# Weight sums moved from GpSimd to VectorE, and a pair's raw weights fetched in the middle of the pair before it

## The chip, the cores and the metric

One core of a Trainium2 chip runs the whole kernel in one launch. The metric is the device time of one execution in microseconds (us). Three runs of the kernel before took 2743.4, 2746.61 and 2750.3 us; the median is 2746.61.

The engines are TensorE (PE), VectorE (DVE), ScalarE (ACT), GpSimd (POOL) and SyncE (SP), which here issues the transfers (DMA). Each runs its own instructions in order and waits for the others by semaphores.

## The reference

One layer of a diffusion backbone over 1024 tokens of width 1024, all in fp32: a half SwiGLU feed-forward, then a token mixing of two branches (a bidirectional matrix LSTM with 4 heads, and a chunked spatial gating) that share one combined input projection, then a second half SwiGLU feed-forward and a final norm.

```
def project(h, shift, scale, g, w_in, sizes):
    hn = modulate(rmsnorm(h, g), shift, scale)
    return split_cols(hn @ w_in[:, :sum(sizes)], sizes)
...
p_lat = project(h, mods[3], mods[4], g_mix[layer], w_in[layer], PROJ_SIZES)
```

`mods` are nine vectors of shifts, scales and gates, made from the conditioning vector by one large product with `w_ada`. The change lies in the combined projection: q, k, v, the gate columns, o, u, vs and two merge gates ga and gb, each 1024 wide apart from the gate columns. A context of 256 tokens goes through the k, v and gate columns as well.

## The kernel before, in words

**The products.** TensorE multiplies fp32 as three products of a rounded high part and a low part: ScalarE casts a 128x512 piece of weights to its high part (L139), VectorE subtracts to get the low part (L140), and TensorE does high-high, high-low and low-high. The result of the two is a ring page. Each 2x2 block product is done by a scheme with seven products in place of eight. Its operands are sums of the four quarters of the weights (a1, b1, a2, b2) and of the features; the feature sums are ready in `FM` before.

**A pair.** `Pair` handles two rows of 128 weights, in two raw pages of 128x1024 (`rawq`, four buffers, so two pairs at a time). It makes 512 output channels' worth of sums in seven steps, p = 1, 7, 2, 4, 5, 6, 3 (for k also a step 8 for the context, after p=1, and context products in steps 1, 2 and 4). A step is 12 matmuls of 128x512. `load` gives a step its operand: p=7 needs b1 := a1 - b1, p=5 needs b2 := b2 - b1 and a1 := a1 + b2, p=3 needs a2 := a2 - b2. Each of these four sums is one 128x512 instruction, made in place on GpSimd (L1184, L1186, L1187, L1189). The one of p=5 overwrites b2, which the step p=4 reads before. The pages are fetched by SyncE at L1181 when p=1 is loaded.

After the products, p=1's sums are copied to px by ScalarE (L1227) and p=7's to py (L1232). Step p=4 then accumulates into the bank that the py copy reads. VectorE adds p=5's bank to py (L1234) and p=6's to px (L1236); p=3 accumulates into the bank that L1234 reads. `emit` makes the results (L1266 on ScalarE, L1268 on VectorE).

**Rows.** `Rows` does the same for v and vs with the tokens in the rows of the result; its sums for p = 7, 6, 5 and 3 are at L1121 to L1127, four of each in each of the two stages.

**The stream.** A step's load, cast and subtraction are done four steps ahead of its matmuls (seven ahead in wo, wga and wgb). The stages in order are: v (rows), gates, k (4 pairs, 1032 to 1137 us), q (4 pairs, 1137 to 1224), o, ga and gb (12 pairs, 1224 to 1482), vs (rows, to 1560) and u (4 pairs, to 1650).

**What else runs beside them.** In k and q, a convolution along the tokens: ScalarE L1299, VectorE L1300 and L1302 on 128x1023, ScalarE L1322, and a store (L1323). From o on, the product with `w_ada`: SyncE fetches pages of 128x512 (L726) and VectorE accumulates them (L735 the first, L737 the others, then L741 and L742). The state C of the LSTM is updated at L1574.

The order on each engine is not that of the program: a scheduler at build orders all instructions by their dependencies and its own estimates.

Of the kernel before, what the change touches and what calls it, by code (L numbers as in the profile page):

```python
# [13 lines left out]
ALU = mybir.AluOpType  # L14
# [35 lines left out]
def build(tc, a, out):  # L50
    nc = tc.nc
    ctx = ExitStack()
    with ctx:
        _build(ctx, tc, nc, a, out)


def _build(ctx, tc, nc, a, out):
    V, S, G, T = nc.vector, nc.scalar, nc.gpsimd, nc.tensor
# [47 lines left out]
    class Weights:  # L106


        def __init__(self, order, name):
            self.c = ExitStack()  # L110
            self.pool = self.c.enter_context(tc.tile_pool(name=name, bufs=1, reuse_waits="tile"))
            self.order = deque(order)
            self.ready = deque()
            self.held = 0

        def load(self):
            n, i, w = self.order.popleft()
            src = a[n][i]
            raw = self.pool.tile([128, w], F32, name="raw", tag="raw", bufs=2)
            nc.sync.dma_start(raw, src)  # L120
            hl = self.pool.tile([128, 2, w], F32R, name="hl", tag="hl", bufs=3)
            split(hl, raw)
            self.ready.append((n, i, hl))
            self.held += 1
# [410 lines left out]
    def xpage(tag, name, shape=(128, 1024), dt=F32):  # L535
        if not xps:
            xps.append(pool("x"))
        return xps[0].tile(list(shape), dt, name=name, tag=tag, bufs=4)

    def rawpg(name="rawq"):  # L540
        return xpage("raw", name)
# [503 lines left out]
    class Stream:  # L1045
# [13 lines left out]
        def fill(self):  # L1059
            while self.q and len(self.ready) < 4 + self.extra:  # L1060
                if isinstance(self.q[0], Bar):
                    if not self.q[0].up:
                        return
                    self.q.popleft()
                    continue
                load, run = self.q.popleft()
                src = load()
                hl = self.ring()
                split(hl, src)
                self.ready.append((run, hl))  # L1070
# [27 lines left out]
    class Rows:  # L1098
# [13 lines left out]
        def load(self, p, k):  # L1112
            if p in (1, 2):
                i = k if p == 1 else k + 4
                if i not in self.r:
                    self.get(i, rawpg if p == 1 else raw2)
                return self.r[i][:, 0:512]
            a1, b1 = self.r[k][:, 0:512], self.r[k][:, 512:1024]
            a2, b2 = self.r[k + 4][:, 0:512], self.r[k + 4][:, 512:1024]
            if p == 7:  # L1120
                G.tensor_tensor(b1, a1, b1, ALU.subtract)  # L1121
            elif p == 6:
                G.tensor_tensor(b2, b2, b1, ALU.subtract)
            elif p == 5:
                G.tensor_tensor(a1, a1, b2, ALU.add)
            elif p == 3:
                G.tensor_tensor(a2, a2, b2, ALU.subtract)  # L1127
            return {7: b1, 4: b2, 6: b2, 5: a1, 3: a2}[p]

        def prod(self, p, k, hl):  # L1130
# [39 lines left out]
    class Pair:  # L1170


        def __init__(self, name, i, emit, ctx_emit=None):
            self.name, self.i, self.emit, self.ctx_emit = name, i, emit, ctx_emit
            self.steps = PSEQ if ctx_emit is None else PSEQ[:1] + (8,) + PSEQ[1:]

        def load(self, p):
            if p == 1:
                self.s = [rawpg() for _ in range(2)]
                for j in range(2):  # L1180
                    nc.sync.dma_start(self.s[j], a[self.name][self.i + j])  # L1181
            a1, a2, b1, b2 = (self.s[j][:, o * 512:(o + 1) * 512] for j in range(2) for o in range(2))
            if p == 7:
                G.tensor_tensor(b1, a1, b1, ALU.subtract)  # L1184
            elif p == 5:
                G.tensor_tensor(b2, b2, b1, ALU.subtract)  # L1186
                G.tensor_tensor(a1, a1, b2, ALU.add)  # L1187
            elif p == 3:
                G.tensor_tensor(a2, a2, b2, ALU.subtract)  # L1189
            return {1: a1, 2: a2, 8: b1, 7: b1, 4: b2, 6: b2, 5: a1, 3: a2}[p]  # L1190

        def prod(self, p, hl):
# [49 lines left out]
    def rows_steps(name, emit, side=(), early=False):  # L1242
        r = Rows(name, emit, early)
        n = 0
        for p in RSEQ:
            for k in range(4):
                st.q.append((lambda p=p, k=k: r.load(p, k), lambda hl, p=p, k=k: r.prod(p, k, hl)))
                n += 1
                if n == 4:
                    st.q.append(r.bar)  # L1250
            if p == 2:
                for load, run in side:
                    st.q.append((lambda load=load: load(r), run))
                    n += 1
        return n, r.bar

    def pair_steps(*args):
        pr = Pair(*args)
        for p in pr.steps:
            st.q.append((lambda p=p: pr.load(p), lambda hl, p=p: pr.prod(p, hl)))  # L1260
        return len(pr.steps)
# [78 lines left out]
    def emit_sig(dram):  # L1340
        def emit(i, j, half, x, pt):
# [7 lines left out]
    hnc = [fl("hnc", "hnc", (128, 2, 256), F32R, 8) for _ in range(NKT)]  # L1349
    nct.queue(smod[:, 1, 1, :], mods[:, 3, 1, :], hnc, gap=(1, 2, 12), cost=1280)  # L1350
    nk = sum(pair_steps("wk", i, emit_kq(ksp, 8), emit_kc) for i in range(0, NKT, 2))
    nq = sum(pair_steps("wq", i, emit_kq(qsp, 0)) for i in range(0, NKT, 2))
    ns = sum(pair_steps(n, i, emit_sig(d_)) for n, d_ in (("wo", osp), ("wga", gasp), ("wgb", gbsp))
             for i in range(0, NKT, 2))
    gpg = t2("gpg")
# [262 lines left out]
    def emit_vs(half, j, m, x, pt):  # L1618
# [4 lines left out]
            V.bn_stats(stv[:, i, 2 * j + c_, :], t[:, c_ * 256:(c_ + 1) * 256])  # L1623
        nc.sync.dma_start(vnsp[i, :, j * 512:(j + 1) * 512], t)

    nvs, barvs = rows_steps("wvs", emit_vs)
    wsr = {}
    vnp = {}
# [435 lines left out]
```

## Time and profile before

| what | us |
|---|---|
| median of three runs (lowest, highest) | 2746.61 (2743.4, 2750.3) |
| span of the profiled execution | 2740.7 |
| median over that span | 5.9 |
| the four pair sums on GpSimd, busy (24 of each) | 36.7, 36.5, 32.7, 32.6 |
| the four row sums on GpSimd, busy (8 of each) | 10.8, 11.2, 12.1, 12.1 |

The profiled execution has no time of its own in the results, only its span, the stretch from its first to its last instruction; the median of the runs lies 5.9 us over it. A row of the timeline reads: start, duration, engine, line, operation, out<-in, shape, and in brackets how long the engine had been idle and which instruction of which engine ended that. A row of the waits reads: total us, times, longest.

### The profile page before, as it was taken

Reading aid. Unit: us, or ns where it says so; the run is one execution under the profiler, and the core shown is the slowest. Engines: PE = TensorE matmul, PEld = TensorE weight load, DVE = VectorE, ACT = ScalarE, POOL = GpSimd, SP = SyncE. Lnnn points to the kernel's source line nnn. Section 1 sums busy time; section 2 is a strip of 40 time slices with the busy share of each in tenths; the row PEclk is TensorE's granted clock in tenths of the full one; section 3 lists DMA queues with packets and bytes.
Section 4 is the critical chain, followed back from the end, with each engine's and each line's share of the span. In section 5 each row is a group of like instructions: output and inputs, shape, how many; then the busy total and the mean of one; then the engine's idle time right before and its main releaser. Section 6 shows DMA issues by size and latency. Waiting matters only on the chain.

```text
span 2740.7 us, 35737 instructions
## 1 busy us (share of the span) xinstructions
PE 2665.6 (97%) x12734; PEld 2212.6 (81%) x12734; DVE 1957.4 (71%) x3305; ACT 1082.5 (39%) x1862; POOL 576.8 (21%) x518
## 2 busy tenths in 40 slices
PE   8899999999999999999999999999999999999998
PEld 4787788788888878877888888888877788888887
DVE  4787887777968746667665678768478866666755
ACT  3563333334436625444434333112245333333432
POOL 0102333220000121232221315443011323230000
PEclk9999999999999999999999999999999999999999
DMA  8851443439668421227554357547341333336645
GB/s 285 276 192 66 167 149 132 146 123 316 223 210 274 142 93 65 93 100 240 175 169 150 108 185 263 194 158 265 116 138 54 127 127 112 131 123 243 210 156 171
DMA packets 199585, 456.74 MB, mean 167 GB/s; under 512 B 20592, under 2 KB 49008, under 8 KB 199408
## 3 DMA queue, kind: packets, MB, share of 16 engines
q1 hardware_dynamic: 199408, 454.47, 48.7%
q8 instruction: 100, 1.64, 0.2%
q14 instruction: 77, 0.63, 0.1%
HBM read 328.95 MB, written 125.51 MB: 166 GB/s over the span
## 4 chain that ended last, share of the span: by engine, by line
PE 49%; DVE 5%; issue 4%; POOL 1%; DMA 1%; ACT 1%; SPq 0%; POOLq 0%; DVEq 0%; ACTq 0%
PE pq L1221 12%; PE qb L376 9%; PE pt L1689 8%; PE po L495 6%; PE qa L376 4%; PE pr L1140 3%; PE pn L1802 2%; PE pu L1529 2%; DVE ring L140 1%; PE pn L1800 1%; PE pkc L1201 1%; DMA adapg<-in_w_ada_dram 1%; POOL rawq L1186 1%; DVE adacc L737 1%; POOL rawq L1187 1%
## 5 line engine op out<-in xcount | busy, mean ns | idle before, releaser
L139 ACT CAST ring<-rawq 128x512 fp32r<-128x512 f32 x432 | 266.4, 620 | 589.7 <-PE qb L376 147.6
L140 DVE TENSOR_TENSOR ring<-rawq,ring 128x512 fp32r<-128x512 f32 x432 | 331.9, 770 | 197.0 <-ACT ring L139 194.8
L495 PE MATMUL po<-gring,wring 128*128 128x512 f32 (+1 forms) x1896 | 424.9, 385 | 0.3 <-DMA gring<-fsp 0.3
L495 PEld LDWEIGHTS po<-gring,wring 128*128 128x128 f32 x1896 | 349.6, 188 | 71.5 <-issue 1.4
L376 PE MATMUL qb<-fc,ring 128*128 128x512 f32 x1440 | 345.7, 394 | 16.1 <-DVE u L396 8.6
L376 PEld LDWEIGHTS qb<-fc,ring 128*128 128x128 f32 x1440 | 272.9, 190 | 76.9 <-DVE y L399 9.8
L376 PE MATMUL qa<-fa,ring 128*128 128x512 f32 x1056 | 253.4, 390 | 0.5 <-ACT ring L139 0.5
L376 PEld LDWEIGHTS qa<-fa,ring 128*128 128x128 f32 x1056 | 197.9, 188 | 42.7 <-ACT ring L139 0.9
L1221 PE MATMUL pq<-fc,ring 128*128 128x512 f32 x864 | 216.8, 400 | 14.4 <-ACT py L1232 9.7
L376 PE MATMUL qb<-fb,ring 128*128 128x512 f32 x984 | 229.5, 389 | 0.0
L376 PEld LDWEIGHTS qb<-fb,ring 128*128 128x128 f32 x984 | 184.7, 188 | 38.4
L1221 PEld LDWEIGHTS pq<-fc,ring 128*128 128x128 f32 x864 | 162.3, 190 | 52.9 <-ACT py L1232 11.6
L139 ACT CAST wring<-rw 128x512 fp32r<-128x512 f32 x154 | 95.7, 622 | 230.3 <-PE po L495 192.3
L1689 PE MATMUL pt<-yp,ring 128*128 128x512 f32 x768 | 184.3, 396 | 0.0
L140 DVE TENSOR_TENSOR wring<-rw,wring 128x512 fp32r<-128x512 f32 x154 | 106.0, 688 | 94.0 <-ACT wring L139 93.8
L1689 PEld LDWEIGHTS pt<-yp,ring 128*128 128x128 f32 x768 | 144.1, 188 | 29.3
L1221 PE MATMUL pq<-fa,ring 128*128 128x512 f32 x576 | 141.0, 392 | 0.2 <-ACT px L1227 0.2
L1221 PE MATMUL pq<-fb,ring 128*128 128x512 f32 x576 | 137.8, 393 | 0.0
L737 DVE SCALAR_TENSOR_TENSOR adacc<-adapg,sc,adacc 128x512 f32<-128x512 f32 x140 | 120.1, 871 | 16.5 <-DMA adapg<-in_w_ada_dram 14.9
L1221 PEld LDWEIGHTS pq<-fb,ring 128*128 128x128 f32 x576 | 107.8, 188 | 22.9 <-PE pu L1570 0.4
L1221 PEld LDWEIGHTS pq<-fa,ring 128*128 128x128 f32 x576 | 107.0, 188 | 23.7 <-ACT px L1227 1.3
L139 ACT CAST ring<-rawt 128x512 fp32r<-128x512 f32 x64 | 39.6, 619 | 185.1 <-PE pt L1689 173.1
(341 smaller groups left out, 4424.7 us busy)
## 6 DMA issues: line engine op xcount, KB each, us to landing
adapg<-in_w_ada_dram SPq DMA_DIRECT2D x144, 256.0 KB, 3.9
fsp<-fhl SPq DMA_DIRECT2D x66, 512.0 KB, 2.9
gring<-fsp SPq DMA_DIRECT2D x66, 512.0 KB, 3.6
raw<-in_w1i_dram SPq DMA_DIRECT2D x44, 512.0 KB, 4.8
graw<-fsp SPq DMA_DIRECT2D x88, 256.0 KB, 3.6
rawq<-in_w1i_dram SPq DMA_DIRECT2D x38, 512.0 KB, 3.9
rawq<-in_w2i_dram SPq DMA_DIRECT2D x38, 512.0 KB, 3.3
fsp<-x SPq DMA_DIRECT2D x66, 256.0 KB, 2.1
```

What stands on the lines that cost most here:

```text
L139: S.copy(hl[:, 0, :], src)
L140: V.tensor_sub(hl[:, 1, :], src, hl[:, 0, :].bitcast(F32))
L376: T.matmul(pt, hl[:, x, sl], pages[p][k][:, y, :], start=first and i == 0, stop=i == 11, skip_group_check=not first)
L495: T.matmul(pt[:, cs], w[:, x, sl], g[:, y, cs], start=grp and kp == 0 and i == 0, stop=kp == NFP - 1 and i == 2, skip_group_check=not grp)
L737: eng.scalar_tensor_tensor(acc, pgt, sc2[:, q, k:k + 1], acc, ALU.mult, ALU.add)
L1140: T.matmul(self.pt[m], pg[:, x, sl], hl[:, y, :], start=first and k == 0 and i == 0, stop=k == 3 and i == 2, skip_group_check=not first)
L1186: G.tensor_tensor(b2, b2, b1, ALU.subtract)
L1187: G.tensor_tensor(a1, a1, b2, ALU.add)
L1221: T.matmul(pt, hl[:, x, k * 128:(k + 1) * 128], pg[k][:, y, :], start=first and k == 0 and i == 0, stop=k == 3 and i == 2, skip_group_chec ...
L1529: T.matmul(pu[:, 0:257], ksl[:, kt * 128:(kt + 1) * 128], wv, start=True, stop=True)
L1689: T.matmul(pt, hl[:, x, k * 128:(k + 1) * 128], pg[:, y, :], start=kh + k + i == 0, stop=kh == 1 and k == 3 and i == 2)
L1802: T.matmul(pn[:, 0:257], qi[:, c_, :], self.C[d][:, c_, :], start=False, stop=c_ == 1)
```

## The change

The eight lines that make the weight sums, four in `Rows.load` and four in `Pair.load`, go from GpSimd (`G`) to VectorE (`V`). And a pair has a method `fetch`, which the pair before it calls at its third step in order (p=2, or p=7 in k); p=1 calls it only if the pages are not there yet. The first pair of k and the first of u still fetch at p=1.

```
-                G.tensor_tensor(b1, a1, b1, ALU.subtract)
+                V.tensor_tensor(b1, a1, b1, ALU.subtract)
...
-
-        def load(self, p):
-            if p == 1:
+            self.s, self.next = None, None
+
+        def fetch(self):
+            if self.s is None:
                 self.s = [rawpg() for _ in range(2)]
                 for j in range(2):
                     nc.sync.dma_start(self.s[j], a[self.name][self.i + j])
+
+        def load(self, p):
+            if p == 1:
+                self.fetch()
+            elif p == self.steps[2] and self.next is not None:
+                self.next.fetch()
             a1, a2, b1, b2 = (self.s[j][:, o * 512:(o + 1) * 512] for j in range(2) for o in range(2))
             if p == 7:
-                G.tensor_tensor(b1, a1, b1, ALU.subtract)
+                V.tensor_tensor(b1, a1, b1, ALU.subtract)
             elif p == 5:
-                G.tensor_tensor(b2, b2, b1, ALU.subtract)
-                G.tensor_tensor(a1, a1, b2, ALU.add)
+                V.tensor_tensor(b2, b2, b1, ALU.subtract)
+                V.tensor_tensor(a1, a1, b2, ALU.add)
             elif p == 3:
-                G.tensor_tensor(a2, a2, b2, ALU.subtract)
+                V.tensor_tensor(a2, a2, b2, ALU.subtract)
+                self.s = ()
...
     def pair_steps(*args):
         pr = Pair(*args)
+        if last[0] is not None:
+            last[0].next = pr
+        last[0] = pr
```

The lines move: L1184, L1186, L1187 and L1189 become L1191, L1193, L1194 and L1196, L1227 and L1232 become L1235 and L1240, L1234 becomes L1242, L1299, L1300, L1302 and L1322 become L1312, L1313, L1315 and L1335, L1268 becomes L1281. Below, names are tiles with the number of their buffer in the build, and the brackets tell which engines are waited for.

On ScalarE, at the first pair of q, before: px is copied (L1227), then p=5's piece is cast (out of raw page 9900, with a wait for GpSimd), then come L1322 of the convolution and the copy of py (L1232).

```order
L1227 COPY px_9980<-pq_9967 128x512 [waits PE_49]
L139 CAST ring_9984<-rawq_9900 128x512 [waits Activation_49,Pool_49]
L1322 ACTIVATE cv_9945<-cv_9945 128x1024 [waits DVE_49,Activation_49]
L1232 COPY py_10003<-pq_9990 128x512 [waits PE_49]
L139 CAST ring_10005<-rawq_9901 128x512
L1322 ACTIVATE cv_9987<-cv_9987 128x1024 [waits DVE_49,Activation_49]
```

The same place now:

```order
L1235 COPY px_9984<-pq_9971 128x512 [waits PE_49]
L1335 ACTIVATE cv_9949<-cv_9949 128x1024 [waits DVE_49,Activation_49]
L1240 COPY py_10007<-pq_9994 128x512 [waits PE_49]
L139 CAST ring_9988<-rawq_9736 128x512 [waits DVE_49]
L139 CAST ring_10009<-rawq_9737 128x512
L1335 ACTIVATE cv_9991<-cv_9991 128x1024 [waits DVE_49,Activation_49]
```

The cast of p=5's piece moved behind L1335 and the py copy; it now waits for VectorE.

On VectorE, at the same pair, before: p=4's subtraction (into ring page 9961), with the convolution around it, and those of p=5, 6 and 3 (9984, 10005 and 10026).

```order
L1300 SCALAR_TENSOR_TENSOR cv_9945<-pre_9939,vec_84,cv_9945 128x1023 [waits DMAHW0_49,Activation_49]
L140 TENSOR_TENSOR ring_9961<-rawq_9901,ring_9961 128x512 [waits Activation_49]
L1302 SCALAR_TENSOR_TENSOR cv_9945<-pre_9939,vec_84,cv_9945 128x1023 [waits DVE_49]
L1300 SCALAR_TENSOR_TENSOR cv_9987<-pre_9858,vec_84,cv_9987 128x1023 [waits DMAHW1_49,Activation_49]
L140 TENSOR_TENSOR ring_9984<-rawq_9900,ring_9984 128x512 [waits PE_49,Activation_49]
L1302 SCALAR_TENSOR_TENSOR cv_9987<-pre_9858,vec_84,cv_9987 128x1023 [waits DVE_49]
L140 TENSOR_TENSOR ring_10005<-rawq_9901,ring_10005 128x512 [waits PE_49,Activation_49]
L140 TENSOR_TENSOR ring_10026<-rawq_9900,ring_10026 128x512 [waits PE_49,Activation_49]
```

The same place now, where p=4's ring page is 9965 and those of p=5, 6 and 3 are 9988, 10009 and 10030:

```order
L1313 SCALAR_TENSOR_TENSOR cv_9949<-pre_9939,vec_84,cv_9949 128x1023 [waits DMAHW0_49,Activation_49]
L140 TENSOR_TENSOR ring_9965<-rawq_9737,ring_9965 128x512 [waits Activation_49]
L1315 SCALAR_TENSOR_TENSOR cv_9949<-pre_9939,vec_84,cv_9949 128x1023 [waits DVE_49]
L1193 TENSOR_TENSOR rawq_9737<-rawq_9737 128x512 [waits DVE_49]
L1313 SCALAR_TENSOR_TENSOR cv_9991<-pre_9862,vec_84,cv_9991 128x1023 [waits DMAHW1_49,Activation_49]
L1194 TENSOR_TENSOR rawq_9736<-rawq_9736,rawq_9737 128x512 [waits DVE_49]
L1315 SCALAR_TENSOR_TENSOR cv_9991<-pre_9862,vec_84,cv_9991 128x1023 [waits DVE_49]
L140 TENSOR_TENSOR ring_9988<-rawq_9736,ring_9988 128x512 [waits PE_49,Activation_49]
L140 TENSOR_TENSOR ring_10009<-rawq_9737,ring_10009 128x512 [waits PE_49,Activation_49]
L1196 TENSOR_TENSOR rawq_9736<-rawq_9736,rawq_9737 128x512
L140 TENSOR_TENSOR ring_10030<-rawq_9736,ring_10030 128x512 [waits PE_49,Activation_49]
```

The two sums of p=5 stand between the convolution's instructions, and the p=5 subtraction is behind the last of these.

On VectorE in the o stage, at the pair whose p=3 starts at 1268.43 us in the profile before, up to its L1234 (py_10778), before:

```order
L735 TENSOR_SCALAR adacc_10805<-adapg_10806,sc2_96 128x512 [waits DMAHW7_49]
L737 SCALAR_TENSOR_TENSOR adacc_10805<-adapg_10830,sc2_96,adacc_10805 128x512 [waits DMAHW2_49,DVE_49]
L140 TENSOR_TENSOR ring2_10802<-rawq_10755,ring2_10802 128x512 [waits PE_49,Activation_49]
L737 SCALAR_TENSOR_TENSOR adacc_10805<-adapg_10858,sc2_96,adacc_10805 128x512 [waits DMAHW3_49,DVE_49]
L140 TENSOR_TENSOR ring2_10827<-rawq_10756,ring2_10827 128x512 [waits Activation_49]
L737 SCALAR_TENSOR_TENSOR adacc_10805<-adapg_10886,sc2_96,adacc_10805 128x512 [waits DMAHW6_49,DVE_49]
L737 SCALAR_TENSOR_TENSOR adacc_10805<-adapg_10909,sc2_96,adacc_10805 128x512 [waits DMAHW7_49,DVE_49]
L1234 TENSOR_TENSOR py_10778<-py_10778,pq_10839 128x512 [waits PE_49]
```

The same place now, up to that pair's last sum (L1196); L1191 is the p=7 sum of the next pair and waits for the two DMAs of its raw pages:

```order
L735 TENSOR_SCALAR adacc_10809<-adapg_10810,sc2_96 128x512 [waits DMAHW7_49]
L1191 TENSOR_TENSOR rawq_10803<-rawq_10802,rawq_10803 128x512 [waits DMAHW2_49,DMAHW0_49]
L737 SCALAR_TENSOR_TENSOR adacc_10809<-adapg_10834,sc2_96,adacc_10809 128x512 [waits DMAHW4_49,DVE_49]
L140 TENSOR_TENSOR ring2_10831<-rawq_10623,ring2_10831 128x512 [waits Activation_49]
L737 SCALAR_TENSOR_TENSOR adacc_10809<-adapg_10862,sc2_96,adacc_10809 128x512 [waits DMAHW5_49,DVE_49]
L1193 TENSOR_TENSOR rawq_10623<-rawq_10623 128x512 [waits DVE_49]
L1242 TENSOR_TENSOR py_10778<-py_10778,pq_10843 128x512 [waits PE_49]
L1194 TENSOR_TENSOR rawq_10622<-rawq_10622,rawq_10623 128x512 [waits DVE_49]
L737 SCALAR_TENSOR_TENSOR adacc_10809<-adapg_10890,sc2_96,adacc_10809 128x512 [waits DMAHW6_49]
L1196 TENSOR_TENSOR rawq_10622<-rawq_10622,rawq_10623 128x512
```

Two of the four L737 that stood ahead of py's sum (L1242) are behind it now; L1191, with its wait for the raw pages, and L1193 stand ahead of it.

On SyncE the two fetches of a pair stand at the same place as before or up to four places earlier. In q the store of a convolution result that stood between them is now ahead of both.

More of the change, by code (lines that the diff above doesn't have):

```diff
@@ L1181, in load @@
                     nc.sync.dma_start(self.s[j], a[self.name][self.i + j])
+        def load(self, p):
[3 more added lines that the diff above has]
+                self.next.fetch()
             a1, a2, b1, b2 = (self.s[j][:, o * 512:(o + 1) * 512] for j in range(2) for o in range(2))
             if p == 7:
-                G.tensor_tensor(b1, a1, b1, ALU.subtract)
+                V.tensor_tensor(b1, a1, b1, ALU.subtract)
             elif p == 5:
-                G.tensor_tensor(b2, b2, b1, ALU.subtract)
-                G.tensor_tensor(a1, a1, b2, ALU.add)
+                V.tensor_tensor(b2, b2, b1, ALU.subtract)
+                V.tensor_tensor(a1, a1, b2, ALU.add)
             elif p == 3:
-                G.tensor_tensor(a2, a2, b2, ALU.subtract)
+                V.tensor_tensor(a2, a2, b2, ALU.subtract)
+                self.s = ()
             return {1: a1, 2: a2, 8: b1, 7: b1, 4: b2, 6: b2, 5: a1, 3: a2}[p]
@@ L1255, in rows_steps @@
         return n, r.bar
+    last = [None]
     def pair_steps(*args):
         pr = Pair(*args)
+        if last[0] is not None:
+            last[0].next = pr
+        last[0] = pr
         for p in pr.steps:
@@ L1624, in emit_vs @@
         nc.sync.dma_start(vnsp[i, :, j * 512:(j + 1) * 512], t)
+    last[0] = None
     nvs, barvs = rows_steps("wvs", emit_vs)
```

## The prediction

> **What bounds the kernel now.** First the page: the span, and how busy each engine is.
>
> ```profile
> span 2740.7 us, 35737 instructions
> PE 2665.6 (97%) x12734; PEld 2212.6 (81%) x12734; DVE 1957.4 (71%) x3305; ACT 1082.5 (39%) x1862; POOL 576.8 (21%) x518
> ```
>
> TensorE is busy for all but 75 us of the span, so a change to VectorE and GpSimd can win only what TensorE waits for them, and what its clock loses behind such waits. The changed lines run from the token-row projection wv to wu. So the next view is TensorE's waits in 985 to 1650 us, by line waited for.
>
> ```profile
> PE pq L1221 <- ACT py L1232: 9.7, 5, 2.4
> PE pq L1221 <- DVE py L1234: 4.7, 5, 1.3
> PE pr L1430 <- DVE bcz L1425: 0.6, 1, 0.6
> ```
>
> Five waits, 9.7 us, are for ScalarE's copy of the p=7 sums (py, L1232): step p=4 accumulates into the bank that this copy reads. Five more, 4.7 us, are for VectorE's L1234, which reads the p=5 bank before p=3 accumulates into it. In TensorE's timeline the first five are these; the first row is an undisturbed step of 12 matmuls.
>
> ```profile
> 1142.89 2.88 PE L1221 MATMUL pq<-fa,ring 128*128 128x512 f32 x12
> 1147.39 3.02 PE L1221 MATMUL pq<-fc,ring 128*128 128x512 f32 x12 [1.61 <-ACT py L1232]
> 1168.92 3.03 PE L1221 MATMUL pq<-fc,ring 128*128 128x512 f32 x12 [2.20 <-ACT py L1232]
> 1190.14 4.59 PE L1221 MATMUL pq<-fc,ring 128*128 128x512 f32 x12 [1.87 <-ACT py L1232]
> 1212.71 3.06 PE L1221 MATMUL pq<-fc,ring 128*128 128x512 f32 x12 [1.61 <-ACT py L1232]
> 1234.89 4.61 PE L1221 MATMUL pq<-fc,ring 128*128 128x512 f32 x12 [2.36 <-ACT py L1232]
> ```
>
> They are p=4 of the four wq pairs and of the first wo pair. Why the copy is late shows in the first of them, in all engines' timeline:
>
> ```profile
> 1140.00 0.69 DVE L140 TENSOR_TENSOR ring<-rawq,ring 128x512 fp32r<-128x512 f32 x1
> 1140.60 1.28 DVE L1302 SCALAR_TENSOR_TENSOR cv<-pre,vec,cv 128x1023 f32<-128x1023 f32 x1
> 1140.76 2.26 POOL L1186 TENSOR_TENSOR rawq<-rawq 128x512 f32<-128x512 f32 x1 [7.83 <-DVE ring L140]
> 1141.80 2.31 DVE L1300 SCALAR_TENSOR_TENSOR cv<-pre,vec,cv 128x1023 f32<-128x1023 f32 x1
> 1143.10 2.15 POOL L1187 TENSOR_TENSOR rawq<-rawq 128x512 f32<-128x512 f32 x1
> 1145.29 0.62 ACT L139 CAST ring<-rawq 128x512 fp32r<-128x512 f32 x1 [4.33 <-POOL rawq L1187]
> 1145.81 1.05 ACT L1322 ACTIVATE cv<-cv 128x1024 f32<-128x1024 f32 x1
> 1146.77 0.57 ACT L1232 COPY py<-pq 128x512 f32<-128x512 f32 x1
> ```
>
> The p=4 split (L140) frees page half b2; GpSimd makes the two p=5 sums in 4.5 us; ScalarE stands 4.33 us at the p=5 cast, and the py copy is queued behind that cast and L1322. The copy ends at 1147.34, TensorE restarts at 1147.39, though the p=7 result was there at about 1143.
>
> **The sum, part by part.**
>
> *The five py waits go.* In the changed order ScalarE does px, L1322 (there L1335), the py copy, and only then the p=5 cast. Estimate for this pair: L1322 needs the first L1302, done at 1141.88, so it ends at 1142.9; the copy needs p=7, done about 0.16 us after its last matmul's successor starts at 1142.89, 1143.05, and ends at 1143.65. TensorE needs it at 1145.61 (1147.39 less 1.78: 1142.89 plus one step of 2.72). Margin 1.9 us. The cast behind it is the next candidate: on VectorE the sums stand between the conv operations, so 1141.88 + 0.69 (L1186) + 1.28 (L1300) + 0.69 (L1187) = 1144.5; cast 1145.1; then L1302 to 1145.8 and L140 to 1146.5, wanted at 1148.33. It too has 1.8 us. So the idle goes: 1.61 + 2.20 + 1.87 + 1.61 + 2.36 = 9.65 us. With it go the long blocks behind: (3.02 + 3.03 + 4.59 + 3.06 + 4.61) less 5 x 2.88 = 3.91 us. Together **-13.6 us**.
>
> Of these 3.91 us, 3.4 are two blocks run at a low clock. The windows view (after the span: TensorE busy, weight loads, VectorE, ScalarE, GpSimd, granted clock) has for the middle of one:
>
> ```profile
> 1192.00:1194.00 2.00, 2.00 (x6) 1.61 (x5) 0.69 (x1) 1.12 (x3) 0.00 (x0) 0.50 0.72 219
> ```
>
> Six matmuls in 2 us at clock 0.50, right behind a 1.87 us wait; the waits of 1.61 and 2.20 us left none. I take the drop as a result of the wait and count it. The Trainium skill ("TensorE: Matmul & The Clock Gate", What's actually happening) halves the clock only after a whole idle window of about 3.4 us. By that rule these waits are too short, the low clock is not theirs and may stay: the sum would be -10.2. The trace has the slow matmuls straight behind two of the waits and disagrees.
>
> *What VectorE takes on.* Rows of the POOL and DVE groups (busy us, mean ns), 900 to 1650:
>
> ```profile
> L1186 POOL TENSOR_TENSOR rawq<-rawq 128x512 f32<-128x512 f32 x24 | 36.7, 1530 | 169.2 <-DVE ring L140 169.2
> L1125 POOL TENSOR_TENSOR rawq<-rawq,raw 128x512 f32<-128x512 f32 x8 | 12.1, 1515 | 0.5
> L1234 DVE TENSOR_TENSOR py<-py,pq 128x512 f32<-128x512 f32 x24 | 16.4, 683 | 20.4 <-PE pq L1221 20.4
> L737 DVE SCALAR_TENSOR_TENSOR adacc<-adapg,sc,adacc 128x512 f32<-128x512 f32 x56 | 53.3, 952 | 11.9 <-DMA adapg<-in_w_ada_dram 10.6 <-DVE ring L140 0.3
> ```
>
> Four sums in each of 24 pairs, and four kinds of 8 in the two row stages, are 128 instructions. VectorE's same-sized add takes 0.683 us: 128 x 0.69 = 88 us, 2.76 per pair. In return VectorE no longer runs beside GpSimd: L737 should fall from 0.95 to 0.75 (its undisturbed row at 1263.00, below), 56 x 0.2 = 11 us; L140 and L1300 give some more. Net some 60 us more on an engine with room, by the windows:
>
> ```profile
> 985.00:1645.00 660.00, 644.88 (x2987) 528.80 (x2986) 435.44 (x670) 277.50 (x475) 161.57 (x115) 0.99 0.42 142
> 1236.00:1482.00 246.00, 241.25 (x1050) 195.99 (x1050) 171.36 (x253) 100.14 (x202) 65.23 (x47) 0.99 0.58 190
> ```
>
> wo to wgb (1236 to 1482) is the tightest place that TensorE still waits in: 171 + 33 (12 pairs) - 12 = 192 of 246 us, 78%. By throughput nothing is lost; what counts is the order in the queue.
>
> *The order in wo to wgb.* The pair whose p=3 starts at 1268.43 is the worst case, since its next raw pages come late:
>
> ```profile
> 1258.14 0.43 SPq L1181 DMA_DIRECT2D rawq<-in_wo_dram  x1
> 1264.01 1.49 POOL L1184 TENSOR_TENSOR rawq<-rawq 128x512 f32<-128x512 f32 x1 [13.05 <-DMA rawq<-in_wo_dram]
> 1259.19 0.48 DVE L735 TENSOR_SCALAR adacc<-adapg,sc 128x512 f32<-128x512 f32 x1
> 1263.00 0.75 DVE L737 SCALAR_TENSOR_TENSOR adacc<-adapg,sc,adacc 128x512 f32<-128x512 f32 x1 [0.34 <-DVE ring L140]
> 1265.33 2.46 DVE L737 SCALAR_TENSOR_TENSOR adacc<-adapg,sc,adacc 128x512 f32<-128x512 f32 x2 [0.97 <-DMA adapg<-in_w_ada_dram]
> 1267.70 0.68 DVE L1234 TENSOR_TENSOR py<-py,pq 128x512 f32<-128x512 f32 x1
> ```
>
> GpSimd waited 13 us for that page at the p=7 sum with nothing behind it that mattered. In the changed order VectorE stands there instead, right behind L735 (done at 1259.67), with two L737, the p=4 split, a p=5 sum and L1234 queued behind it, and TensorE behind L1234. With the page at 1264.01: 0.69 + 0.75 + 0.69 + 0.75 + 0.69 later, L1234 starts at 1267.6, against 1267.70 now. Neutral, since L1234 is already late there (TensorE waits 0.8 us). Two pairs later, where L1234 is not late:
>
> ```profile
> 1303.95 1.29 POOL L1184 TENSOR_TENSOR rawq<-rawq 128x512 f32<-128x512 f32 x1 [13.69 <-DMA rawq<-in_wga_dram]
> 1309.69 0.69 DVE L1234 TENSOR_TENSOR py<-py,pq 128x512 f32<-128x512 f32 x1 [2.21 <-PE pq L1221]
> ```
>
> From the page at 1303.95 to L1234 at 1309.69 are 5.7 us; the changed queue puts eight instructions there (four sums, three splits, one L737), 8 x 0.7 = 5.6 us, and TensorE's p=6 gives some 2 us of grace. I take the 4.7 us of L1234 waits as unchanged: **0**. Bounds: -4.7 (the L737 pairs beside GpSimd shrink), +11 (0.9 us for each of the 12 pairs, two of the three sums ahead of it less half of one).
>
> *The rest.* The wk stage puts three sums between the gate scans ahead of L1430: 0 to +2 us (3 x 0.69), taken as **+0.5**, because the scans lose GpSimd's company. The row sums and wu have no wait on py or the sums now: 0, bounds -0.6 and +2; the cover is the four steps that the ring holds.
>
> *The fetch.* It moves the pages' DMA four places in SyncE's queue at most; the scheduler already issues it when the buffers come free, long ahead of use:
>
> ```profile
> 1148.90 0.33 SPq L1181 DMA_DIRECT2D rawq<-in_wq_dram  x1
> 1179.95 2.88 PE L1221 MATMUL pq<-fa,ring 128*128 128x512 f32 x12
> ```
>
> That page is first used by TensorE 31 us later, and no wait on a raw page stands among TensorE's. Worth **0**, bounds -1 and +2 (stores of cv now go ahead of it).
>
> Sum: -13.6 + 0.5 = -13.1 us on a profiled execution whose span is 2740.7, 5.9 us below the median of 2746.61; what lies around the span stays. **2733.5 us.**
>
> **The rivals.**
> *A: L1234's waits go as well.* Beside GpSimd's sums, L737 took 3.40 us for two at 1287.40, just ahead of a late L1234:
>
> ```profile
> 1287.40 3.40 DVE L737 SCALAR_TENSOR_TENSOR adacc<-adapg,sc,adacc 128x512 f32<-128x512 f32 x2 [0.79 <-DMA adapg<-in_w_ada_dram]
> ```
>
> Without GpSimd it is 1.5, and TensorE's 1.23 us wait goes. Against it: the sums put back as much. All five gone: 2733.5 - 4.7 = 2728.8. The Trainium skill ("SBUF — State Buffer", Who interferes with whom) says that of two such instructions the second stands until the first is done. The rows above show both long at once (2.26 and 2.31 us); either way the wait ends when the sums leave GpSimd.
>
> *B: VectorE becomes what TensorE waits for.* The sums ahead of L1234 cost 0.9 us in each of 12 pairs: -13.1 + 11 gives 2744.5, within 0.3%. For it: L1234 already decides five waits. Against: 22% of idle, and the slack worked out above.
>
> *C: slower.* VectorE's wait for a raw page holds the L737 behind it; L737 frees the page buffers for SyncE's next w_ada transfers; the next raw page is queued behind those on SyncE. If that loop costs each of the 12 pairs the 2.15 us that two such issues take now ahead of the fetch of 1258.14,
>
> ```profile
> 1255.94 2.15 SPq L726 DMA_DIRECT2D adapg<-in_w_ada_dram  x2
> ```
>
> it is 26 us: 2746.6 - 13.1 + 26 = 2759.5. It decides the sign from 1.1 us per pair on, and is measurably slower from 1.8.
>
> *D: the copies stay late* because the first L1302 or p=7 ends later than I think: half the gain, 2740.
>
> **How the numbers follow.** Forecast 0.53, A 0.10, B 0.15, C 0.13, D 0.09. What a measurement here can tell from no change is 0.3%, 8.2 us: faster is below 2738.4, slower above 2754.8. Faster: 0.53 + 0.10 = 0.63; same: B and D, 0.24; slower: 0.13. The range reaches from A (2728.8, less 1.8 for the small bounds: 2727) through D and B to 2748 (B with wk's and wu's bounds); C and a little of A are left out.
>
> **What would show it.** Right: no TensorE wait on the py copy in 1137 to 1240, that copy ended by 1.5 us or more before p=4, no block above 3.1 us there, clock 1.00 in it; L1234's waits between 2 and 8 us; L737 near 750 ns; the sums at 690 ns on VectorE. Wrong: waits on VectorE's py of more than 12 us in 1236 to 1482, long VectorE idle ended by raw-page DMAs with TensorE idle 5 us later (C), or py waits that remain (D).

## The result, and the profile after

The changed kernel took 2724.49 us (median of four runs, 2721.01 to 2726.14), the kernel before 2745.01 us beside it (four runs, 2741.55 to 2750.3). The ratio is 0.9919, with an interval from 0.9907 to 0.9932: 22 us faster (19 to 26), where 13 were forecast; the two medians alone lie 20.5 us apart. The direction and the larger mechanism were as forecast. The time lies below the range, because a second group of waits went that the forecast had left standing.

The page of the kernel after, span and engines:

```profile
span 2724.4 us, 35676 instructions
PE 2662.2 (98%) x12734; PEld 2211.3 (81%) x12734; DVE 1988.1 (73%) x3433; ACT 1083.9 (40%) x1862; POOL 392.8 (14%) x390
```

GpSimd has lost 184 us of work, VectorE has gained 31. TensorE's waits in 985 to 1650 us are now:

```profile
PE pu L1583 <- ACT wv L1566: 1.1, 1, 1.1
PE pq L1229 <- DVE py L1242: 0.3, 1, 0.3
PE pm L1660 <- DMA vnp<-vnsp: 0.3, 1, 0.3
```

The five waits on the py copy (9.7 us) are gone, as forecast. So are nearly all of the waits on VectorE's py sum, 4.7 us before and 0.3 now, which the forecast had left standing. In the kernel before, two L737 stand right ahead of that sum in all five places where TensorE waited, and they are stretched each time (2.44 to 3.40 us for the two); undisturbed, two take 1.5 us. The prediction shows two of these places (2.46 and 3.40 us); two more:

```profile
1245.69 2.44 DVE L737 SCALAR_TENSOR_TENSOR adacc<-adapg,sc,adacc 128x512 f32<-128x512 f32 x2
...
1350.70 2.98 DVE L737 SCALAR_TENSOR_TENSOR adacc<-adapg,sc,adacc 128x512 f32<-128x512 f32 x2 [1.21 <-DMA adapg<-in_w_ada_dram]
```

Four landmarks of TensorE's timeline tell what each stage gave; each is the first matmul of a stretch, in the kernel before: of the v rows, of q, of the second half of the first o pair, of the vs rows.

```profile
917.62 4.97 PE L1140 MATMUL pr<-ring,fa 128*128 128x512 f32 x21
...
1137.45 2.88 PE L1221 MATMUL pq<-fa,ring 128*128 128x512 f32 x12
...
1239.34 2.91 PE L1221 MATMUL pq<-fb,ring 128*128 128x512 f32 x12
...
1482.77 17.39 PE L1140 MATMUL pr<-ring,fa 128*128 128x512 f32 x76
```

The same four in the kernel after:

```profile
921.04 4.95 PE L1140 MATMUL pr<-ring,fa 128*128 128x512 f32 x21
...
1140.60 2.88 PE L1229 MATMUL pq<-fa,ring 128*128 128x512 f32 x12
...
1228.13 3.24 PE L1229 MATMUL pq<-fb,ring 128*128 128x512 f32 x12
...
1467.91 17.39 PE L1140 MATMUL pr<-ring,fa 128*128 128x512 f32 x76
```

The differences are +3.4, +3.2, -11.2 and -14.9 us, and -16.3 at the end. The first is a stretch that the change does not touch: this execution was 3.4 us slower there. v rows and k: -0.3. q with the first o pair: -14.4 (forecast: -13.6). o to gb: -3.7 (forecast: 0). From vs on: -1.4. Together -19.7 us from the v rows on.

The first q pair in the kernel after, rows of VectorE and ScalarE and the first of p=4 on TensorE, to be laid beside the rows from 1140.00 of the kernel before:

```profile
1143.14 0.69 DVE L140 TENSOR_TENSOR ring<-rawq,ring 128x512 fp32r<-128x512 f32 x1
1143.74 1.29 DVE L1315 SCALAR_TENSOR_TENSOR cv<-pre,vec,cv 128x1023 f32<-128x1023 f32 x1
1144.93 0.69 DVE L1193 TENSOR_TENSOR rawq<-rawq 128x512 f32<-128x512 f32 x1
1145.12 1.06 ACT L1335 ACTIVATE cv<-cv 128x1024 f32<-128x1024 f32 x1 [1.01 <-DVE cv L1315]
1145.53 1.29 DVE L1313 SCALAR_TENSOR_TENSOR cv<-pre,vec,cv 128x1023 f32<-128x1023 f32 x1
1146.23 0.59 ACT L1240 COPY py<-pq 128x512 f32<-128x512 f32 x1
1146.73 0.69 DVE L1194 TENSOR_TENSOR rawq<-rawq 128x512 f32<-128x512 f32 x1
1147.46 1.14 ACT L139 CAST ring<-rawq 128x512 fp32r<-128x512 f32 x2 [0.64 <-DVE rawq L1194]
...
1148.76 1.52 PE L1229 MATMUL pq<-fc,ring 128*128 128x512 f32 x6
```

The copy ends at 1146.82 and TensorE starts p=4 at 1148.76, on time: 1.94 us of margin, where 1.9 was worked out. The p=5 cast now stands behind the copy. No conv instruction is stretched: L1313 takes 1.29 us, where L1300 took 2.31 beside GpSimd.

The pair of o that the prediction took as its worst case, VectorE, after:

```profile
1249.33 0.48 DVE L735 TENSOR_SCALAR adacc<-adapg,sc 128x512 f32<-128x512 f32 x1
1251.66 0.69 DVE L1191 TENSOR_TENSOR rawq<-rawq 128x512 f32<-128x512 f32 x1 [1.85 <-DMA rawq<-in_wo_dram]
1252.95 0.75 DVE L737 SCALAR_TENSOR_TENSOR adacc<-adapg,sc,adacc 128x512 f32<-128x512 f32 x1 [0.60 <-DMA adapg<-in_w_ada_dram]
1253.62 0.69 DVE L140 TENSOR_TENSOR ring<-rawq,ring 128x512 fp32r<-128x512 f32 x1
1254.22 0.75 DVE L737 SCALAR_TENSOR_TENSOR adacc<-adapg,sc,adacc 128x512 f32<-128x512 f32 x1
1254.89 0.69 DVE L1193 TENSOR_TENSOR rawq<-rawq 128x512 f32<-128x512 f32 x1
1255.49 0.68 DVE L1242 TENSOR_TENSOR py<-py,pq 128x512 f32<-128x512 f32 x1
```

VectorE does stand at L1191 for the raw page, but for 1.85 us and not 4.3, and the py sum is done at 1256.17, ahead of p=3 at 1256.53. The queue is the one that the order showed; everything in it takes its undisturbed time. The sum starts 3.8 us behind the page, where 3.6 was worked out. What differs is the page: it is there 4.9 us ahead of p=3, and in the kernel before it was there 3.7 us ahead of the time at which TensorE wanted p=3 (1268.43 less the wait of 0.76). Why it came earlier is not shown; without the early fetch (below) this pair has no wait either.

### The profile page after: what moved, and what is told of

Same layout as the page of the kernel before. It is cut to its first block, busy times and chain, and to the rows that moved or that the text cites. A ratio compares the mean times of both kernels' runs of the same rounds, so it can differ in the third digit from the quotient of the medians.

```text
span 2724.4 us, 35676 instructions
## 1 busy us (share of the span) xinstructions
PE 2662.2 (98%) x12734; PEld 2211.3 (81%) x12734; DVE 1988.1 (73%) x3433; ACT 1083.9 (40%) x1862; POOL 392.8 (14%) x390
## 4 chain that ended last, share of the span: by engine, by line
PE 77%; DVE 11%; DMA 6%; issue 4%; ACT 2%; POOL 1%; SPq 0%; POOLq 0%; DVEq 0%; ACTq 0%
PE qb L376 18%; PE po L495 13%; PE pq L1229 12%; PE pt L1703 9%; PE qa L376 8%; PE pr L1140 6%; DMA raw<-in_w1i_dram 2%; PE pc L1011 2%; DVE ring L140 2%; PE pn L1816 2%; PE pu L1542 2%; PE adr L796 1%; DVE hl L140 1%; PE pkc L1209 1%; DMA adapg<-in_w_ada_dram 1%
## 5 line engine op out<-in xcount | busy, mean ns | idle before, releaser
L140 DVE TENSOR_TENSOR ring<-rawq,ring 128x512 fp32r<-128x512 f32 x432 | 317.4, 739 | 146.5 <-ACT ring L139 144.1
L140 DVE TENSOR_TENSOR wring<-rw,wring 128x512 fp32r<-128x512 f32 x154 | 105.7, 687 | 93.5 <-ACT wring L139 93.4
L737 DVE SCALAR_TENSOR_TENSOR adacc<-adapg,sc,adacc 128x512 f32<-128x512 f32 x140 | 108.6, 789 | 9.9 <-DMA adapg<-in_w_ada_dram 9.1
```

Source lines behind the costliest of these rows:

```text
L140: V.tensor_sub(hl[:, 1, :], src, hl[:, 0, :].bitcast(F32))
L737: eng.scalar_tensor_tensor(acc, pgt, sc2[:, q, k:k + 1], acc, ALU.mult, ALU.add)
```

## The experiments

Each kernel ran 5 to 11 times beside the kernel before; all numbers are ratios to it, with intervals. "Full change" is the kernel after. Twelve kernels in three groups: which part does it, why the copy was late, and why the py sum no longer is.

**Sums without the early fetch.** The two lines of `load` that fetch for the next pair are taken out again.

```
-            elif p == self.steps[2] and self.next is not None:
-                self.next.fetch()
```

> The eight sums on VectorE, the pair's fetch back at its own p=1. Theory S (the sums alone do it): about 0.992 of the kernel before, as the full change; TensorE's waits on py by ScalarE and by VectorE both under 1 us. Theory F (the early fetch brought the part that was not forecast, the end of the waits on VectorE's py sum): about 0.9945, with 3 to 6 us of waits on the py sum left in o to gb.

0.9926 (0.9913 to 0.9940), no wait on py at all in TensorE's list. The sums alone do it.

**The early fetch alone.** All eight lines are back on `G`.

> The early fetch alone, all sums still on GpSimd. Theory S: 1.000, the same waits on py as before (9.7 and 4.7 us). Theory F: about 0.998, with the waits on the py sum gone or halved and those on the py copy as before.

1.0003 (0.9995 to 1.0012), waits 10.0 and 4.3 us on py as before. The fetch is worth nothing that can be measured, as forecast.

**Sums on VectorE for k and q; for o, ga and gb; for the rows and u.** The engine is chosen by name, the early fetch stays:

```
-                V.tensor_tensor(b1, a1, b1, ALU.subtract)
+                (V if self.name in ("wk", "wq") else G).tensor_tensor(b1, a1, b1, ALU.subtract)
```

> The early fetch, and the sums on VectorE for the pairs of k and q only; o to gb, u and the rows stay on GpSimd. Theory S, and the forecast's sum: the four waits on the py copy in q go with their slow matmuls, 10 us, so about 0.9963; the fifth, of the first o pair, and the 4.7 us on the py sum stay. If the copies are late for another reason than the p=5 cast ahead of them: 1.000.

0.9958 (0.9946 to 0.9971), 11.5 us: the four waits of q are gone, the fifth (2.2 us) stays. The waits on the py sum were 6.8 us here.

> The early fetch, and the sums on VectorE for the pairs of o, ga and gb only. Theory S: the fifth wait on the py copy goes (4 us with its slow matmuls) and the 4.7 us on the py sum go, so about 0.997; w_ada accumulation (L737) near 750 ns. If the sums ahead of L1242 cost more than GpSimd's company did (the forecast's rival of a VectorE queue that is too long): 0.9985 or above, with the waits on the py sum at 5 us or more.

0.9969 (0.9956 to 0.9982), 8.5 us. Of TensorE's waits on py, 850 to 1650 us, only those on the four copies of q are left (the second row is the next in the list):

```profile
PE pq L1229 <- ACT py L1240: 7.3, 4, 2.0
PE pu L1583 <- ACT wv L1566: 1.1, 1, 1.1
```

> The early fetch, and the sums on VectorE for the two row stages and the pairs of u only. Both theories of the extra gain: 0.9990 to 1.0005; the waits on py as before (9.7 and 4.7 us). If these stages carried a part of the gain that the waits do not show: 0.998 or below.

0.9996 (0.9987 to 1.0004): nothing that can be told. The three parts add up, 11.5 + 8.5 + 1.1 = 21.1 us, to the full change's 22 within their intervals.

**Why the copy was late: the py copy on VectorE, all sums on GpSimd.**

```
                 self.y = t2("py")
-                S.copy(self.y, pt)
+                V.tensor_copy(self.y, pt)
```

> The kernel before, all sums on GpSimd and no early fetch, with one line changed: the copy of the p=7 sums to py is made by VectorE instead of ScalarE. Theory: the copy was late only because it stood behind the p=5 cast in ScalarE's queue; then the five waits and the slow matmuls behind them go, 13.6 us or 0.995, without any sum moved, and the 4.7 us on the py sum stay. Rival: GpSimd's slow p=5 sums hold the p=5 operand itself, and the wait moves to that ring page: 0.998 to 1.000.

1.0017 (1.0009 to 1.0026): slower, neither as the theory nor as the rival had it. The timeline of its first q pair shows why:

```profile
1145.56 2.15 POOL L1187 TENSOR_TENSOR rawq<-rawq 128x512 f32<-128x512 f32 x1
...
1147.74 0.62 ACT L139 CAST ring<-rawq 128x512 fp32r<-128x512 f32 x1 [4.33 <-POOL rawq L1187]
...
1148.40 1.10 DVE L140 TENSOR_TENSOR ring<-rawq,ring 128x512 fp32r<-128x512 f32 x1 [1.83 <-ACT ring L139]
...
1149.42 0.68 DVE L1232 COPY py<-pq 128x512 f32<-128x512 f32 x1
...
1150.15 4.61 PE L1221 MATMUL pq<-fc,ring 128*128 128x512 f32 x12 [1.92 <-DVE py L1232]
```

The scheduler put the copy (L1232) behind the p=5 subtraction (L140) in VectorE's queue, and that waits for the same GpSimd sums through ScalarE's cast. The copy changed its engine, not what stood ahead of it.

**The p=5 cast on GpSimd, the copy left on ScalarE.** The cast that ScalarE stood at is taken out of its queue; the sums stay on GpSimd.

```
                 src = load()
                 hl = self.ring()
-                split(hl, src)
+                if gcast[0]:
+                    G.tensor_copy(hl[:, 0, :], src)
+                    V.tensor_sub(hl[:, 1, :], src, hl[:, 0, :].bitcast(F32))
+                else:
+                    split(hl, src)
```

`gcast[0]` is set at p=5 of a pair.

> The kernel before, with one thing changed: the cast of the p=5 operand of a pair (the first half of its split) is made by GpSimd, right behind its two sums, instead of by ScalarE. ScalarE then has no wait for the p=5 sums ahead of the py copy in q; all sums and GpSimd's company stay, with some 24 us more of it. Theory of the queue: the four waits on the py copy in q go with their slow matmuls (10 us), the first o pair's may stay; the py sum's stay or grow by 1 to 3 us: 0.9965 to 0.998. Rival (the p=5 operand itself is late, as in the run with the copy on VectorE): the waits move to the ring page of p=5, 0.999 to 1.001.

0.9974 (0.9964 to 0.9984). TensorE's list has no wait on the py copy left, in q or in o:

```profile
PE pq L1228 <- DVE py L1241: 6.6, 6, 1.5
PE pq L1228 <- ACT ring L139: 1.4, 1, 1.4
```

So the copies were late because of the cast ahead of them in the queue, and they are on time without one sum moved. From the first matmul of q to the third landmark this kernel gains the same 14.4 us as the full change (1140.32 to 1227.85 us, against 1137.45 to 1239.34 before). Only 7 us show in the time: from there to the vs rows it loses 8.6 us against the kernel before, in waits that were not there (on ring pages, 1.4 and 1.0 us, among others) and longer ones on the py sum. GpSimd has more work there (72 us in 1236 to 1482, 65 before); how much of the loss is due to that is not shown.

**Only the two p=5 sums on VectorE.** In the kernel before, `G` becomes `V` in the two lines of p=5 in `Pair.load`.

> The kernel before with only the two p=5 sums of each pair on VectorE; p=7, p=3 and the rows stay on GpSimd, no early fetch. Theory: the five waits on the py copy go (13.6 us), and GpSimd keeps two of its four instructions in each pair, so a part of the waits on the py sum stays, 1 to 4 us: 0.9935 to 0.995. If the p=5 sums were all that mattered: 0.992.

0.9928 (0.9914 to 0.9941): nearly all of it, 20 us, with 2 of 4 sums moved. The waits on the py sum are 1.5 us, and L737 is at 810 ns, between 952 and 749. GpSimd still works 38 us in 1225 to 1470, beside VectorE, and costs little by it.

**Room on VectorE: the load of the sums doubled.** Behind each sum, a second instruction of its size:

```
                 V.tensor_tensor(b1, a1, b1, ALU.subtract)
+                V.tensor_tensor(idle, b1, idle, ALU.subtract)
```

> The full change, and behind each of the 96 pair sums one more VectorE subtraction of the same size into a tile that nobody reads: 66 us more on VectorE. Theory of room (VectorE has a fifth of its time free and the order holds): 0.992 to 0.994, waits on py under 3 us. Theory of the queue (each instruction ahead of the py sum costs 0.3 us or more of TensorE in each of 12 pairs, as in the forecast's rival): 0.997 or above.

0.9920 (0.9908 to 0.9933): 66 us more on VectorE cost nothing. In its windows VectorE is the third engine after the span, at 207 of 245 us in o to gb and 82 of 90 in q, with TensorE full beside it:

```profile
1225.00:1470.00 245.00, 244.67 (x1075) 199.58 (x1074) 207.13 (x349) 101.41 (x204) 0.00 (x0) 1.00 0.60 196
1135.00:1225.00 90.00, 89.67 (x397) 73.50 (x396) 82.40 (x114) 50.54 (x71) 0.00 (x0) 1.00 0.34 117
```

**GpSimd's company put back.** The full change, and idle work on GpSimd in each pair of o, ga and gb, behind the p=5 sums:

```
                 V.tensor_tensor(a1, a1, b2, ALU.add)
+                if self.name in ("wo", "wga", "wgb"):
+                    for _ in range(3):
+                        G.tensor_tensor(idle, b2, idle, ALU.subtract)
```

> The full change, and in each pair of o, ga and gb three GpSimd subtractions of 128x512 out of b2 into a tile that nobody reads, behind the p=5 sums, where GpSimd's own sums ran before. If GpSimd's company beside L737 made the py sum late: L737 back at 900 ns or more, 3 to 7 us of waits on the py sum, 0.9935 to 0.995. If it was the order (two of the four w_ada accumulations now stand behind the py sum): 0.992, under 1 us of waits, whatever L737 takes.

0.9970 (0.9959 to 0.9980): 36 GpSimd instructions whose results nobody uses take back 14 of the 22 us. Its windows (VectorE 200.5 us, fewer than with the doubled load, TensorE 233), and VectorE with GpSimd ahead of one py sum:

```profile
1225.00:1470.00 245.00, 233.17 (x999) 186.71 (x998) 200.53 (x294) 97.99 (x198) 57.43 (x35) 0.99 0.56 182
```

```profile
1232.29 0.49 DVE L735 TENSOR_SCALAR adacc<-adapg,sc 128x512 f32<-128x512 f32 x1 [1.57 <-DMA adapg<-in_w_ada_dram]
...
1235.67 5.16 POOL L1199 TENSOR_TENSOR idle<-rawq,idle 128x512 f32<-128x512 f32 x3 [7.91 <-issue]
1236.27 1.75 DVE L737 SCALAR_TENSOR_TENSOR adacc<-adapg,sc,adacc 128x512 f32<-128x512 f32 x1
1237.94 0.68 DVE L1247 TENSOR_TENSOR py<-py,pq 128x512 f32<-128x512 f32 x1
...
1238.67 4.41 PE L1234 MATMUL pq<-fc,ring 128*128 128x512 f32 x12 [3.50 <-DVE py L1247]
```

One L737 takes 1.75 us in place of 0.75, right ahead of the py sum, and TensorE waits. That is 1.0 of the 3.50 us; 1.57 more are VectorE's wait at L735, further up its queue, for a page of `w_ada`. In this pair the company also did something else than stretch. SyncE stood 1.1 us until GpSimd had read the raw page that the next fetch overwrites:

```profile
SPq L1184 <- POOL idle L1199: 1.1, 1, 1.1
```

Transfers of `w_ada` stand behind that fetch in SyncE's order, so a part of this one wait may come from there; the next run has no such wait. L737 came to 812 ns in the mean, not to the 900 expected; the waits on the py sum were 7.1 us.

The order in VectorE's queue, the rival, is out: by the traces all 3433 instructions of VectorE stand in the same order in the full change, in this run and in the two that follow (apart from one that clears `idle`).

**The same company earlier,** behind the p=7 sum and out of b1.

> The full change, with the same three idle GpSimd subtractions in each pair of o, ga and gb as in the run with GpSimd's company, but out of b1 behind the p=7 sum, some steps before the py sum instead of right ahead of it. If the place decides (stretched instructions right ahead of the py sum): 0.992 to 0.9945, waits on the py sum under 3 us. If the amount decides (VectorE's time in the stage): 0.997, as there.

0.9963 (0.9951 to 0.9976), L737 at 973 ns, waits on the py sum 5.9 us: close to the run above, and no fetch waits for the company. The place that I chose decides little; the two intervals overlap, so a small part of it stays open. The mean of L737 does not decide it alone either: at 810 ns the run with two sums moved lost little, at 812 the company run lost 14 us. There GpSimd worked 57 us in 1225 to 1470 and VectorE 201, with two sums moved 38 and 178. Which of the two counts more no run tells.

**GpSimd work that only writes,** at the place of the company:

```
+                    G.tensor_tensor(idle[:, 0:16], b2[:, 0:16], idle[:, 0:16], ALU.subtract)
+                    for _ in range(6):
+                        G.memset(idle, 0.0)
```

> The full change, with GpSimd work at the place of the run with GpSimd's company, but work that only writes: in each pair of o, ga and gb one subtraction of 128x16 out of b2, and behind it six memsets of 128x512 of a tile that nobody reads. If GpSimd holds VectorE up by its reads alone: 0.992, L737 near 750 ns, no waits on the py sum. If by any access: 0.994 or above, L737 at 800 ns or more. What the Trainium skill states on it (page SBUF — State Buffer, Who interferes with whom): a VectorE instruction with two inputs in SBUF contends with a GpSimd instruction that reads SBUF, not with one that only writes it; by that, 0.992.

0.9919 (0.9906 to 0.9932), the full gain, with 38 us of memsets on GpSimd beside VectorE. L737's group row:

```profile
L737 DVE SCALAR_TENSOR_TENSOR adacc<-adapg,sc,adacc 128x512 f32<-128x512 f32 x56 | 42.0, 749 | 7.0 <-DMA adapg<-in_w_ada_dram 6.3
```

VectorE's order is that of the run that lost 14 us, and GpSimd is busy for 43 us in 1225 to 1470, against 57 there and 47 in the run with the company earlier, which lost 12. What differs most is that GpSimd reads nothing of size out of SBUF. (Memsets are also another kind of instruction; reads of another kind were not run.) So it is not that GpSimd is busy: it is its reads beside VectorE's two-input instructions. The Trainium skill ("SBUF — State Buffer", Who interferes with whom) says just this, and the runs agree: 749 ns beside memsets, 812 and 973 beside subtractions.

## Why the prediction was right and wrong

- *The five py waits go, -13.6:* right in place, mechanism and size. The stretch gave -14.4 us, the margin of the first copy came out at 1.94 us for 1.9, and the run with the p=5 cast on GpSimd shows the queue to be the cause: the same -14.4 without a sum moved.
- *The slow matmuls behind the waits, counted at 3.4 of these:* they went with the waits; no block of p=4 in q is longer than 2.88 us after. But not every wait had one, nor does every slow block have a wait (below), and the kernel after has a new one in k, of 1.4 us. What sets the clock down stays open, so that the size came out is in part luck.
- *The fetch, 0:* right (1.0003).
- *VectorE has room:* right, and by more than was claimed: another 66 us of such work cost nothing.
- *Rows, u and the gate scans, +0.5:* close in size, but by luck. The rows with u gave nothing measurable, and v rows and k together -0.3. That is the sum of two things that the forecast did not count: TensorE's waits on VectorE there, 0.8 us at L1287 and 0.6 at L1430, went instead of growing, and the slow block in k cost 1.4. The run with the doubled load, at clock 1.00 in 1030 to 1036, gained 1.9 us in the same stretch (from 917.63 to 1135.57).
- *The order in wo to wgb, "I take the 4.7 us of L1234 waits as unchanged: 0":* **this is the step that failed.** It gave -3.7 us in the trace; rival A, at a chance of 0.10, had its whole -4.7. I worked out that the sums ahead of the py sum put back what the stretched L737 give up, 1267.6 for 1267.70 in one pair and 5.6 us for 5.7 in another, and called it even. The two are not alike. The scheduler has an instruction of VectorE in its order: two of the four L737 went behind the py sum, and even a doubled load found its places. What GpSimd's reads add to an instruction of VectorE shows in no order, and is there again in whatever run has them. Put back beside the sums on VectorE they cost 14 and 12 us for 36 GpSimd instructions, in the same order of VectorE's queue; GpSimd work without reads costs nothing. That the 3.7 us of the kernel before are the same thing rests on its rows: two stretched L737 ahead of each of the five waits, and L737 at 749 ns in the mean after.
- *What VectorE takes on, net 60 us in all, 21 in o to gb (33 less 12):* too high. It is 31 us in all. In o to gb VectorE is at 185.4 of 245 us in the kernel after, against 171.4 of 246 before: net 14. The relief was 19, not 12; I had counted L737 alone, though the L140 rows of the same view have it too (767 ns there before, 687 after).
- *The time:* 2733.5 forecast, 2724.5 measured. Of the 9.0 us, 3.7 are the py sum, 0.8 the copies, 0.8 the rows and k with the 0.5 counted for them, 1.4 from vs on (not explained further), and 1.6 that the median of before is now 2745.0. The remaining 0.7 is within what single executions differ by. Even rival A's 2728.8 lies 4.3 us above the time: it had the py sum, and nothing of the other four.

Rivals B and C, where VectorE becomes the bound or stands for raw pages, fell: it does stand for them, 20.4 us in o to gb, and TensorE does not notice. So did D, with the waits on the copies.

One reading of the prediction needs a word. It has two stretched rows "both long at once" (L1186, 2.26 us, and L1300, 2.31). That does not speak against one engine standing until the other is done. L1302 ends at 1141.88, L1186 at 1143.02, L1300 at 1144.11, and L1187, the next on GpSimd, at 1145.25: each ends 1.1 us behind one of the other engine, a little less than the 1.28 that each takes undisturbed. The rows fit two engines that take turns, with the time of standing counted in the row.

## What to carry to other kernels

Two engines that slow each other can cost more than the sum of their busy times tells: price a move between them by the rows that are stretched now, on both engines and in every group of the view, and not by one instruction put in for one taken out. When a copy or a cast is late, read what stands ahead of it in its engine's queue and what that waits for; moving it to another engine helps only if it does not land behind the same operand there. And where an in-order engine has time to spare (here a quarter, and still a sixth with the doubled load), more work on it can be free, if a scheduler may place it.

## What the runs showed of the hardware

GpSimd memsets of 128x512 (526 ns each) leave VectorE's two-input instructions alone; GpSimd subtractions out of SBUF stretch them (single L737 of 1.75 us for 0.75) and are stretched themselves (1.55 and 1.71 us in the mean of the two company runs, for 1.29 undisturbed).

TensorE's clock fell for some 3 us behind some waits of 1.8 us or more, and not behind others: with waits on the copies of q of 1.61 to 1.99 us in the run of o to gb alone, no block was slow (3.01 us, where the two slow ones before took 4.59 and 4.61). It also fell with no wait at all. In the kernel after, TensorE is busy throughout 1034 to 1039 us, behind 20 matmuls of only 16 columns:

```profile
1032.00:1034.00 2.00, 2.00 (x20) 1.87 (x18) 0.00 (x0) 0.00 (x0) 0.00 (x0) 1.00 0.00 0
1034.00:1035.50 1.50, 1.50 (x12) 1.47 (x12) 0.60 (x3) 0.51 (x3) 0.00 (x0) 0.81 0.05 11
1036.00:1039.00 3.00, 3.00 (x10) 2.33 (x9) 0.31 (x2) 2.55 (x4) 0.00 (x0) 0.61 0.00 0
```

The same stretch ran at 1.00 in the kernel before. The three drops named here cost 1.4 to 1.7 us each, and they come in some kernels' profiles and not in others'. Together with the stretch ahead of 917 us, which differed by 3.4 us between the two profiles though nothing was changed there, this is why one profile's span could not have given the second digit of the gain.
